# One score matmul for two chunks in recurrence levels 1 to 16, with half of each half's tokens in turned order

## The chip, the cores and the metric

The kernel runs on one core of one Trainium2 chip. The metric is the device time of one execution in microseconds (us); the time of a kernel is the median of its runs. The engines are PE (matrix multiply, with PEld for the loading of its weights), DVE (vector), ACT (scalar), POOL (general) and SP (which issues most DMAs). Each engine works off its own list of instructions in order and waits on semaphores for the others.

## The reference

A decoder layer for 2048 tokens of width 1024: two groups of heads in parallel on the normed input, an output projection, and a gated MLP with a causal convolution. What matters here is the recurrence of the first group, four heads with keys and values of width 128, in chunks:

```python
def step(state, inp):
    qi, ki, vi, gi = inp
    b = jnp.cumsum(gi, axis=2)
    rel = b[:, :, :, None, :] - b[:, :, None, :, :]
    decay = jnp.exp(jnp.where(causal, rel, -jnp.inf))
    scores = jnp.einsum('bhtk,bhsk,bhtsk->bhts', qi, ki, decay)
    intra = jnp.einsum('bhts,bhsv->bhtv', scores, vi)
    inter = jnp.einsum('bhtk,bhkv->bhtv', qi * jnp.exp(b), state)
    ...
    return new_state, intra + inter
```

A score of query t and key s is a sum over 128 channels, each weighted with the decay of that channel between s and t. The second group is attention of eight heads with a window of 128 tokens.

## The kernel before, in words

Activations stand transposed, channels on the 128 partitions and tokens along the free axis. The kernel goes through the 2048 tokens in two halves of 1024 (`hf`). In each half a mixing stage comes first: for each head `h` of 0 to 3, `hgrn` computes the recurrence and `attend` two heads of attention, both written as generators whose pieces the main loop calls in turn. After it come the output projection (`out_proj`, tile `pop`), the MLP (`gate_up`, `down`). Projections go through `unit` (L195): weights and activations are split into a high and a low part, and three matmuls of 128x512 stand for each pair of tiles. `project_v` (tile `pvv`, matmuls of 256 columns) makes the values for two heads at a time, beside heads 0 and 2.

In `hgrn` the scores of a chunk of 128 tokens are built by levels m = 1, 2, 4, ... 64. At level m the tokens are cut into pairs of blocks of m: queries of the later block meet keys of the earlier one. For that the kernel keeps Q and K with the decay inside the block already multiplied in, and F with the decay of whole blocks. Per level (L445 to L475):

- for m < 32, PE multiplies, for each of the 8 chunks, all 128 keys of the chunk as weights (`K`, float32) with the 64 queries of the later blocks (L454). The result `plev` is 128x64 a chunk, one PSUM bank for the 8; only the places where key block and query block belong together are wanted;
- DVE multiplies the later blocks of Q (L462) and the earlier blocks of K (L463) by F, which prepares the next level, and forms the next F (L465);
- DVE copies the wanted places, given by the mask `lmask`, from `plev` into the scores `ST` (L470, a predicated copy);
- levels 32 and 64 have blocks of their own (L460) and are copied by ACT (L474).

The diagonal (`pdiag`, L428) comes before, the transposes of K (`pkn`), the state products (`pu`, L491) and the output (`po`) after.

The matmuls of a level read Q and K before DVE overwrites them, and those of the next level read what DVE wrote. `plev` comes from a pool of two PSUM banks. The order on each engine isn't that of the code: the framework's scheduler sets it when the kernel is built, and puts projection or attention work between the levels. In head 3 of each half little is left for that: the first output projections (`pop`), the attention scores (`psc`), and their transposes (`ppt`, `poT`).

Of the kernel before, what the change touches and what calls it, by code (L numbers as in the profile page):

```python
# [45 lines left out]
def hymba_layer(ctx: ExitStack, tc: tile.TileContext, a: dict, out: bass.AP):  # L46
# [49 lines left out]
    def constants():  # L96
# [10 lines left out]
        for m in LEVELS[:5]:  # L107
            t = cp.tile([P, 64], F32, name=f"lmask{m}")
# [4 lines left out]
            nc.gpsimd.affine_select(out=t, in_=t, compare_op=ALU.is_ge, fill=0.0, base=m - 1,  # L113
                                    pattern=[[2 * m, nb], [0, m]], channel_multiplier=-1)
            C.lmask[m] = t
# [146 lines left out]
    def load(hf, X, stage, W=None):  # L262

        st = Stats(inv_tile())
        for kt in range(KT):
            first = W is not None and kt == 0
            if W is not None and kt < 2:
                W.append(prep(a["w_att"][ATT_J + kt], parts=(slice(0, P), slice(P, D)) if first else (slice(0, D),)))
            x = stage()
            X.append(new_x())  # L270
            for c in [bs for _, bs in halves()] if first else [slice(0, HALF)]:
                nc.sync.dma_start(x[:, c], a["xT"][kt, :, hf * HALF + c.start:hf * HALF + c.stop])
                split(x[:, c], nmw[:, kt:kt + 1], dst=[t[:, c] for t in X[kt]])
            st.add(x)
            yield st

    def first_unit(X, W, i, then={}):
        return unit(W[i] if W else a["w_att"][ATT_J + i], X, "kv", then=then)

    def rows(kv):  # L280
        return slice(kv * HD, (kv + 1) * HD)

    def att_keys(hf, kv, invb, p):
# [10 lines left out]
        for jj, dst in ((ATT_J, kT), (ATT_J + 1, vT)):  # L294
            o = kv[jj - ATT_J]
            for b, bs in halves():
                nc.vector.tensor_tensor(dst[:, bs], o[b], invb[:, bs], op=ALU.mult)
                nc.scalar.activation(dst[:, bs], dst[:, bs], AF.Identity, bias=C.battn[:, jj:jj + 1])
# [15 lines left out]
    def attend(hf, j, X, invb, KS, V, mix, p):  # L314
# [3 lines left out]
        for b, bs in halves():  # L318
            nc.vector.scalar_tensor_tensor(qT[:, bs], o[b], 0.125, invb[:, bs], op0=ALU.mult, op1=ALU.mult)
            nc.scalar.activation(qT[:, bs], qT[:, bs], AF.Identity, bias=C.bq[:, j:j + 1])  # L320
# [83 lines left out]
    def hgrn(hf, h, X, invb, vs, WG, mix, p, fu=None):  # L404
# [28 lines left out]
        def gate():  # L433
            gu = unit(WG.get(h, a["w_g"][h]), X, "g")
            s = p.tile([P, HALF], F32, tag="f", name="sg", bufs=2)
            for b, bs in halves():
                nc.vector.tensor_tensor(q[:, bs], gu[b], invb[:, bs], op=ALU.mult)
                nc.scalar.activation(s[:, bs], q[:, bs], AF.Sigmoid)
                nc.vector.tensor_tensor(q[:, bs], q[:, bs], s[:, bs], op=ALU.mult)
# [5 lines left out]
        for m in LEVELS:  # L445
            nb = HALF // (2 * m)
            nbc = 64 // m
            Qv = Q.rearrange("p (b w m) -> p b w m", w=2, m=m)
            Kv = K.rearrange("p (b w m) -> p b w m", w=2, m=m)
            Fv = F.rearrange("p (b w) -> p b w", w=2)  # L450
            pl = ps("hg", "plev")
            if m < 32:
                for c in range(TT):
                    mm = nc.tensor.matmul(pl[:, c * 64:(c + 1) * 64], K[:, c * P:(c + 1) * P],  # L454
                                          Qv[:, c * nbc:(c + 1) * nbc, 1], start=True, stop=True)
# [6 lines left out]
            nc.vector.tensor_tensor(Qv[:, :, 1], Qv[:, :, 1], Fv[:, :, 0:1].to_broadcast([P, nb, m]), op=ALU.mult)  # L462
            nc.vector.tensor_tensor(Kv[:, :, 0], Kv[:, :, 0], Fv[:, :, 1:2].to_broadcast([P, nb, m]), op=ALU.mult)  # L463
            Fn = p.tile([P, nb], F32, tag=f"F{m}", name=f"F{m}", bufs=1)
            nc.vector.tensor_tensor(Fn, Fv[:, :, 0], Fv[:, :, 1], op=ALU.mult)  # L465
            F = Fn
            if m < 32:
                dst = ST.rearrange("p c (b w m) -> p c b w m", w=2, m=m)[:, :, :, 1]
                mk = C.lmask[m].bitcast(U32).rearrange("p (b m) -> p b m", m=m)
                nc.vector.copy_predicated(dst, mk.unsqueeze(1).to_broadcast([P, TT, nbc, m]),  # L470
                                          pl.rearrange("p (c b m) -> p c b m", c=TT, m=m))
                continue
# [529 lines left out]
def _layout(i):  # L1002
# [3 lines left out]
    def cols(w, idx):  # L1006
# [54 lines left out]
```

## Time and profile before

| | us |
|---|---|
| runs of the kernel, three | 2253.62, 2253.84, 2255.33 |
| median | 2253.84 |
| the profiled execution: span from first to last instruction (it has no other time of its own) | 2251.9 |
| PE idle in the span (span less busy time) | 38.0 |
| level matmuls L454, busy (640 records) | 83.5 |
| Q and K products L462 and L463 of all levels, busy | 76.9 |
| predicated copies L470, busy (40) | 38.0 |

A profile comes from one execution, recorded by the hardware. Busy time of matmuls overlaps, since they are pipelined: how long a group holds PE is read from the start of its first matmul to the start of the next work. A float32 matmul leaves two records, each with a weight load. "Granted clock" is the share of its full clock that PE was given.

### The profile page before, as it was taken

To read this page: it belongs to the slowest core of one execution; us is meant where nothing else is said; L and a number is where in the kernel's file an instruction comes from. 1 tells how busy PE (TensorE), PEld (TensorE's weight loads), DVE (VectorE), ACT (ScalarE), POOL (GpSimd) and SP (SyncE) were. 2 spreads that over 40 slices of the span, in tenths; PEclk is the share of its full clock that TensorE was granted. 3 is DMA by queue.
4 is the path that set the end of the run, shared out by engine and by line. 5 is a ranking of instruction groups with operands and counts; after the bars stand their busy time and mean duration, and the time that the engine had idled before them with its cause. 6 is when DMAs were issued, how large, how long until landed. Compare 5 with 4: busy or idle time off the path is not lost.

```text
span 2251.9 us, 29785 instructions
## 1 busy us (share of the span) xinstructions
PE 2213.9 (98%) x11622; PEld 1862.1 (83%) x11622; DVE 1639.2 (73%) x2458; ACT 1024.6 (45%) x1781; POOL 7.2 (0%) x27
## 2 busy tenths in 40 slices
PE   8999999999999999999999999999999999999997
PEld 6988987778888888888889889887788888888887
DVE  6567467688888887885855665676888878887766
ACT  5345344454444444435724344435544444443353
POOL 1000000000000000000000000000000000000000
PEclk9999998999999999999999999989999999999999
DMA  4101002222323234974630101113232322359643
GB/s 151 38 29 38 29 29 75 94 85 84 118 88 122 89 122 134 360 254 148 207 122 29 38 29 29 53 51 121 67 114 97 115 92 98 107 179 390 225 136 127
DMA packets 89997, 254.19 MB, mean 113 GB/s; under 512 B 11008, under 2 KB 13184, under 8 KB 89856
## 3 DMA queue, kind: packets, MB, share of 16 engines
q1 hardware_dynamic: 87552, 251.17, 32.6%
q8 instruction: 91, 1.49, 0.3%
q10 hardware_dynamic: 2304, 1.12, 0.2%
q14 instruction: 50, 0.41, 0.1%
HBM read 195.10 MB, written 57.15 MB: 112 GB/s over the span
## 4 chain that ended last, share of the span: by engine, by line
PE 92%; DVE 4%; ACT 2%; DMA 2%; issue 1%; SPq 0%; DVEq 0%; ACTq 0%
PE X L674 7%; PE X L675 7%; PE X L676 7%; PE pop L195 6%; PE hq L195 4%; PE q L195 4%; PE f L195 4%; PE g L195 4%; PE Y L674 3%; PE Y L675 3%; PE Y L676 3%; PE pdx L856 3%; PE pdx L858 3%; PE pdx L857 3%; PE plev L454 3%; PE pdy L857 3%
## 5 line engine op out<-in xcount | busy, mean ns | idle before, releaser
L551 ACT CAST whi<-raw 128x1024 fp32r<-128x1024 f32 x88 | 92.6, 1053 | 118.6 <-PE X L675 72.8
L675 PE MATMUL X<-T,whi 128*128 128x512 f32 x352 | 137.8, 391 | 0.0
L674 PE MATMUL X<-T,whi 128*128 128x512 f32 x352 | 137.2, 390 | 0.0
L676 PE MATMUL X<-T,wlo 128*128 128x512 f32 x352 | 137.0, 389 | 0.0
L740 DVE SCALAR_TENSOR_TENSOR y<-ga,cw,y 128x1024 f32<-128x1024 f32 x88 | 112.6, 1280 | 25.4 <-ACT y L738 25.3
L176 ACT CAST whi<-raw 128x1024 fp32r<-128x1024 f32 (+2 forms) x61 | 63.0, 1036 | 123.8 <-PE q L195 59.1
L552 DVE TENSOR_TENSOR wlo<-raw,whi 128x1024 fp32r<-128x1024 f32 x88 | 107.3, 1219 | 0.0
L680 ACT COPY u<-X 128x512 f32<-128x512 f32 x88 | 51.6, 586 | 113.0 <-PE X L676 112.8
L552 DVE TENSOR_TENSOR xld<-raw,xhd 128x1024 fp32r<-128x1024 f32 x72 | 80.9, 1132 | 22.4 <-ACT xhd L551 22.0
L454 PEld LDWEIGHTS plev<-Q,K 128*128 128x128 f32 x640 | 82.8, 206 | 9.3 <-DVE K L463 4.5
L551 ACT CAST xhd<-raw 128x1024 fp32r<-128x1024 f32 x72 | 69.6, 978 | 45.9 <-DMA raw<-act0T 17.6
L454 PE MATMUL plev<-Q,K 128*128 128x64 f32 x640 | 83.5, 287 | 6.1 <-DVE K L463 6.1
L195 PE MATMUL pop<-XL,whi 128*128 128x512 f32 x256 | 84.5, 395 | 0.7 <-DVE XL L207 0.7
L195 PE MATMUL pop<-XH,wlo 128*128 128x512 f32 x256 | 84.4, 394 | 0.8 <-DVE wlo L177 0.8
L195 PE MATMUL pop<-XH,whi 128*128 128x512 f32 x256 | 84.3, 400 | 0.2
L462 DVE TENSOR_TENSOR Q<-Q,F 128x512 f32<-128x512 f32 x48 | 33.1, 690 | 67.9 <-PE plev L454 39.1
L177 DVE TENSOR_TENSOR wlo<-raw,whi 128x1024 fp32r<-128x1024 f32 (+2 forms) x61 | 73.0, 1202 | 9.3 <-ACT whi L176 9.2
L674 PEld LDWEIGHTS X<-T,whi 128*128 128x128 f32 x352 | 66.1, 188 | 14.2 <-ACT u L680 0.6
L676 PEld LDWEIGHTS X<-T,wlo 128*128 128x128 f32 x352 | 66.1, 188 | 14.2 <-issue 0.5
L675 PEld LDWEIGHTS X<-T,whi 128*128 128x128 f32 x352 | 66.1, 188 | 14.0 <-issue 0.5
L856 PE MATMUL pdx<-xhd,hid 128*128 128x512 f32 x192 | 74.5, 391 | 1.9 <-ACT hid L551 1.0
L674 PE MATMUL X<-T,Sh 128*128 128x512 f32 x176 | 70.1, 398 | 5.2 <-ACT s L680 5.2
(356 smaller groups left out, 6603.0 us busy)
## 6 DMA issues: line engine op xcount, KB each, us to landing
wr<-in_w_down SPq DMA_DIRECT2D x90, 512.0 KB, 5.5
raw<-in_w_gate SPq DMA_DIRECT2D x44, 512.0 KB, 3.6
raw<-in_w_up SPq DMA_DIRECT2D x44, 512.0 KB, 3.6
raw<-act0T SPq DMA_DIRECT2D x20, 512.0 KB, 6.5
raw<-act1T SPq DMA_DIRECT2D x20, 512.0 KB, 5.0
act0B<-y SPq DMA_DIRECT2D x33, 256.0 KB, 2.4
act1B<-y SPq DMA_DIRECT2D x33, 256.0 KB, 2.4
raw<-in_w_out SPq DMA_DIRECT2D x16, 512.0 KB, 4.0
```

Of the source, the lines that this page charges most:

```text
L177: nc.vector.tensor_tensor(lo[:, c], raw[:, c], hi[:, c].bitcast(F32), op=ALU.subtract)
L195: nc.tensor.matmul(o[b], w, x[:, bs], start=f, stop=l)
L454: mm = nc.tensor.matmul(pl[:, c * 64:(c + 1) * 64], K[:, c * P:(c + 1) * P], Qv[:, c * nbc:(c + 1) * nbc, 1], start=True, stop=True)
L551: nc.scalar.copy(h, src)
L552: (eng or nc.vector).tensor_tensor(l, src, h.bitcast(F32), op=ALU.subtract)
L674: nc.tensor.matmul(o, wh[:, ws], xh, start=i == 0 and not more, stop=False, skip_group_check=more)
L675: nc.tensor.matmul(o, wh[:, ws], xl, start=False, stop=False, skip_group_check=more)
L676: nc.tensor.matmul(o, wl[:, ws], xh, start=False, stop=i == 3, skip_group_check=more)
L740: nc.vector.scalar_tensor_tensor(y, g[:, w:w + HALF], C.cw[:, ft, w:w + 1], y, op0=ALU.mult, op1=ALU.add)
L856: nc.tensor.matmul(o, wh[:, i, c], ah[:, i, cols], start=f, stop=False, skip_group_check=more)
L857: nc.tensor.matmul(o, wh[:, i, c], al[:, i, cols], start=False, stop=False, skip_group_check=more)
L858: nc.tensor.matmul(o, wl[:, i, c], ah[:, i, cols], start=False, stop=l, skip_group_check=more)
```

## The change

It has four parts.

1. The input of each half is permuted on the host (`xP`): of its second 512 tokens each block of 32 is turned, so that token r stands at place 31 - r. The order of the blocks stays. What leaves the recurrence or feeds attention (keys, values, queries, gates, and the output `pot`) is turned back while DVE evacuates it from PSUM, by a view with a negative step (`blocks`). Levels 32 and 64 see whole blocks and stay as they were.
2. In a turned block the earlier keys of a pair stand in the second place and the later queries in the first. So in chunk u of the first 512 tokens and chunk u + 4 of the second the wanted keys lie in opposite blocks. ACT gathers them into one tile `G` (128 keys, 64 of each chunk, for each of 4 pairs of chunks), and one matmul takes these as weights and the 64 queries of both chunks as 128 columns: 4 matmuls a level in place of 8. `G` has two buffers.
3. The masks get a second side, the products of Q and K take the blocks of both kinds in one instruction each, K now before Q.
4. The scratch area of dynamic DMA is set to 2048.

```diff
+            t = cp.tile([P, 2, 64], F32, name=f"lmask{m}")
...
-            nc.gpsimd.affine_select(out=t, in_=t, compare_op=ALU.is_ge, fill=0.0, base=0,
-                                    pattern=[[-2 * m, nb], [0, m]], channel_multiplier=1)
-            nc.gpsimd.affine_select(out=t, in_=t, compare_op=ALU.is_ge, fill=0.0, base=m - 1,
-                                    pattern=[[2 * m, nb], [0, m]], channel_multiplier=-1)
+            for side in range(2):
+                ts = t[:, side]
+                nc.gpsimd.affine_select(out=ts, in_=ts, compare_op=ALU.is_ge, fill=0.0, base=-side * m,
+                                        pattern=[[-2 * m, nb], [0, m]], channel_multiplier=1)
+                nc.gpsimd.affine_select(out=ts, in_=ts, compare_op=ALU.is_ge, fill=0.0, base=m - 1 + side * m,
+                                        pattern=[[2 * m, nb], [0, m]], channel_multiplier=-1)
...
-                nc.sync.dma_start(x[:, c], a["xT"][kt, :, hf * HALF + c.start:hf * HALF + c.stop])
+                nc.sync.dma_start(x[:, c], a["xP"][kt, :, hf * HALF + c.start:hf * HALF + c.stop])
...
+    def blocks(t, turn=False):
+        v = t.rearrange("p (g r) -> p g r", r=32)
+        return v[:, :, ::-1] if turn else v
+
+    def across(t, base, dims):
+        v = t[:, :]
+        return bass.AP(v.tensor, v.offset + base, [list(v.ap[0])] + dims)
...
-                nc.vector.tensor_tensor(q[:, bs], gu[b], invb[:, bs], op=ALU.mult)
+                nc.vector.tensor_tensor(blocks(q[:, bs], b), blocks(gu[b]), blocks(invb[:, bs]), op=ALU.mult)
...
             if m < 32:
-                for c in range(TT):
-                    mm = nc.tensor.matmul(pl[:, c * 64:(c + 1) * 64], K[:, c * P:(c + 1) * P],
-                                          Qv[:, c * nbc:(c + 1) * nbc, 1], start=True, stop=True)
-                marks[m] = mm
+                n, nu = 64 // m, TT // 2
+                far, near = [[512 - m, 2], [P, nu], [2 * m, n], [1, m]], [[512 + m, 2], [P, nu], [2 * m, n], [1, m]]
+                G = p.tile([P, 512], F32, tag="G", name="G", bufs=2)
+                nc.scalar.copy(across(G, 0, [[m, 2], [P, nu], [2 * m, n], [1, m]]), across(K, 0, near))
+                for u in range(nu):
+                    marks[m] = nc.tensor.matmul(across(pl, u * 64, [[256, 2], [1, 64]]), G[:, u * P:(u + 1) * P],
+                                                across(Q, u * P + m, [far[0]] + far[2:]), start=True, stop=True)
+                nf = P // m
+                Kv, Qv = across(K, 0, near), across(Q, m, far)
+                Fk = across(F, 1, [[4 * nf - 1, 2], [nf, nu], [2, n], [0, m]])
+                Fq = across(F, 0, [[4 * nf + 1, 2], [nf, nu], [2, n], [0, m]])
+                nc.vector.tensor_tensor(Kv, Kv, Fk, op=ALU.mult)
+                nc.vector.tensor_tensor(Qv, Qv, Fq, op=ALU.mult)
...
-                dst = ST.rearrange("p c (b w m) -> p c b w m", w=2, m=m)[:, :, :, 1]
-                mk = C.lmask[m].bitcast(U32).rearrange("p (b m) -> p b m", m=m)
-                nc.vector.copy_predicated(dst, mk.unsqueeze(1).to_broadcast([P, TT, nbc, m]),
-                                          pl.rearrange("p (c b m) -> p c b m", c=TT, m=m))
+                mk = C.lmask[m].bitcast(U32).rearrange("p s t -> p (s t)")
+                nc.vector.copy_predicated(across(ST.rearrange("p c t -> p (c t)"), m, far),
+                                          across(mk, 0, [[64, 2], [0, nu], [m, n], [1, m]]),
+                                          pl.rearrange("p (s u b m) -> p s u b m", s=2, u=nu, m=m))
...
-            nc.vector.scalar_tensor_tensor(g[:, bs], pt, C.hgw, g[:, bs], op0=ALU.mult, op1=ALU.mult)
+            nc.vector.scalar_tensor_tensor(blocks(g[:, bs]), blocks(pt, b), C.hgw, blocks(g[:, bs]),
+                                           op0=ALU.mult, op1=ALU.mult)
...
+        "xP": x[np.where(ar(S) // 512 % 2, ar(S) ^ 31, ar(S))].T.reshape(KT, P, S),
...
-    nc = bacc.Bacc("TRN2", target_bir_lowering=False, num_devices=1)
+    nc = bacc.Bacc("TRN2", target_bir_lowering=False, num_devices=1, dynamic_dma_scratch_size=2048)
```

Keys, values and queries of attention are evacuated through `blocks` in the same way as the gate above.

What the scheduler made of it is shown at two places. The first is head 0 of the first half, from the diagonal on. DVE before the change (each row: line, operation, written tile, read tiles, size; `hg` and `f` tiles are the head's, `att` and `ql` the attention's, `wlo` a weight split):

```order
L429 TENSOR_TENSOR ST<-pdiag,ident 128x512 x2
L462 TENSOR_TENSOR Q<-Q,f 128x512
L463 TENSOR_TENSOR K<-K,f 128x512
L470 COPY_PREDICATED ST<-lmask_287,plev 128x512
L319 SCALAR_TENSOR_TENSOR att_700<-q_650,invb 128x512
L319 SCALAR_TENSOR_TENSOR att_700<-q_651,invb 128x512
L177 TENSOR_TENSOR wlo<-raw,whi 128x1024
L332 TENSOR_TENSOR ql<-att_700,qh 64x512
L462 TENSOR_TENSOR Q<-Q,F_548 128x256x2
L463 TENSOR_TENSOR K<-K,F_548 128x256x2
```

DVE there with the change:

```order
L442 TENSOR_TENSOR ST<-pdiag,ident 128x512 x2
L473 TENSOR_TENSOR K<-K,f 128x2x256
L473 TENSOR_TENSOR K<-K,F_556 128x2x128x2
L474 TENSOR_TENSOR Q<-Q,f 128x2x256
L491 COPY_PREDICATED ST<-lmask_287,plev 128x2x256
L473 TENSOR_TENSOR K<-K,F_568 128x2x64x4
L331 SCALAR_TENSOR_TENSOR att_700<-q_650,invb 128x512
L331 SCALAR_TENSOR_TENSOR att_700<-q_651,invb 128x16x32
L179 TENSOR_TENSOR wlo<-raw,whi 128x1024
L474 TENSOR_TENSOR Q<-Q,F_556 128x2x128x2
L491 COPY_PREDICATED ST<-lmask_293,plev 128x2x128x2
```

The K products have moved one level or two ahead of the Q products, and the second evacuation of a query tile is in blocks of 32. ACT at the same place with the change (the copies `G<-K` are new, the rest stood there in nearly the same order):

```order
L320 COPY V<-pv 128x512
L178 CAST whi<-raw 128x1024
L465 COPY G<-K 128x2x128x2
L465 COPY G<-K 128x2x64x4
L178 CAST whi<-raw 128x1024
L333 ACTIVATE att_700<-att_700,bq 128x512 x2
L343 CAST qh<-att_700 64x512
L344 CAST qh<-att_700 64x512
L465 COPY G<-K 128x2x32x8
L343 CAST qh<-att_700 64x512
L344 CAST qh<-att_700 64x512
```

The copies for m = 2 and 4 stand together, ahead of the level that uses them. On PE this head had 32 `pvv` matmuls between two level groups; it has 27 now.

The second place is head 3 of the first half, from the Q product of the second level on. DVE before the change (`sc`, `m`, `es` and `den` belong to the softmax of attention):

```order
L462 TENSOR_TENSOR Q<-Q,F_3112 128x256x2
L463 TENSOR_TENSOR K<-K,F_3112 128x256x2
L470 COPY_PREDICATED ST<-lmask_291,plev 128x256x2
L358 TENSOR_TENSOR m<-m,sinkb 128x8
L360 TENSOR_TENSOR es<-sinkb,m 128x8
L368 TENSOR_TENSOR den<-den,es 128x8
L361 TENSOR_SCALAR m<-m 128x8
L369 RECIPROCAL den<-den 128x8
L370 TENSOR_TENSOR sc<-sc,den 128x1024
L462 TENSOR_TENSOR Q<-Q,F_3126 128x128x4
```

DVE there with the change, from the first Q product on:

```order
L474 TENSOR_TENSOR Q<-Q,f 128x2x256
L209 TENSOR_TENSOR XL<-att_2214,XH 128x1024
L491 COPY_PREDICATED ST<-lmask_287,plev 128x2x256
L365 COPY_PREDICATED sc<-own,psc 128x256
L452 TENSOR_TENSOR hg_2912<-hg_2912,sg 128x512
L365 COPY_PREDICATED sc<-own,psc 128x256
L452 TENSOR_TENSOR hg_2912<-hg_2912,sg 128x512
L473 TENSOR_TENSOR K<-K,F_3090 128x2x128x2
L371 TENSOR_TENSOR m<-m,sinkb 128x8
L474 TENSOR_TENSOR Q<-Q,F_3090 128x2x128x2
L491 COPY_PREDICATED ST<-lmask_293,plev 128x2x128x2
L365 COPY_PREDICATED sc<-own,psc 128x256 x2
```

Behind these stand the softmax's `es`, and then the K product, the Q product and the predicated copy of the third level. The normalisation of `sc`, which stood between the second and the third Q product, has moved behind the levels of m = 4 and 8.

More of the change, by code (lines that the diff above doesn't have):

```diff
@@ L296, in att_keys @@
             for b, bs in halves():
-                nc.vector.tensor_tensor(dst[:, bs], o[b], invb[:, bs], op=ALU.mult)
+                nc.vector.tensor_tensor(blocks(dst[:, bs], b), blocks(o[b]), blocks(invb[:, bs]), op=ALU.mult)
                 nc.scalar.activation(dst[:, bs], dst[:, bs], AF.Identity, bias=C.battn[:, jj:jj + 1])
@@ L318, in attend @@
         for b, bs in halves():
-            nc.vector.scalar_tensor_tensor(qT[:, bs], o[b], 0.125, invb[:, bs], op0=ALU.mult, op1=ALU.mult)
+            nc.vector.scalar_tensor_tensor(blocks(qT[:, bs], b), blocks(o[b]), 0.125, blocks(invb[:, bs]),
+                                           op0=ALU.mult, op1=ALU.mult)
             nc.scalar.activation(qT[:, bs], qT[:, bs], AF.Identity, bias=C.bq[:, j:j + 1])
@@ L461, in hgrn @@
                                          Q[:, c * P + s0 + m:c * P + s0 + 2 * m], start=True, stop=True)
-            nc.vector.tensor_tensor(Qv[:, :, 1], Qv[:, :, 1], Fv[:, :, 0:1].to_broadcast([P, nb, m]), op=ALU.mult)
-            nc.vector.tensor_tensor(Kv[:, :, 0], Kv[:, :, 0], Fv[:, :, 1:2].to_broadcast([P, nb, m]), op=ALU.mult)
+                Fv = F.rearrange("p (b w) -> p b w", w=2)
+                nc.vector.tensor_tensor(Qv[:, :, 1], Qv[:, :, 1], Fv[:, :, 0:1].to_broadcast([P, nb, m]), op=ALU.mult)
+                nc.vector.tensor_tensor(Kv[:, :, 0], Kv[:, :, 0], Fv[:, :, 1:2].to_broadcast([P, nb, m]), op=ALU.mult)
+            Fv = F.rearrange("p (b w) -> p b w", w=2)
             Fn = p.tile([P, nb], F32, tag=f"F{m}", name=f"F{m}", bufs=1)
@@ L523, in hgrn @@
                 nc.tensor.transpose(pt[:, i * P:(i + 1) * P], on[:, 4 * b + i], ident)
-            nc.vector.scalar_tensor_tensor(g[:, bs], pt, C.hgw, g[:, bs], op0=ALU.mult, op1=ALU.mult)
+            nc.vector.scalar_tensor_tensor(blocks(g[:, bs]), blocks(pt, b), C.hgw, blocks(g[:, bs]),
+                                           op0=ALU.mult, op1=ALU.mult)
             if h == HG - 1:
```

7 lines of the change are left out of this document (2 added, 5 removed).

## The prediction

> **What bounds the kernel now.** I read the page's busy table first, then the busy time by stage, then who waited for whom.
>
> ```profile
> span 2251.9 us, 29785 instructions
> PE 2213.9 (98%) x11622; PEld 1862.1 (83%) x11622; DVE 1639.2 (73%) x2458; ACT 1024.6 (45%) x1781; POOL 7.2 (0%) x27
> ```
> ```profile
> 56.00:120.00 64.00, 64.00 (x488) 59.58 (x487) 34.47 (x61) 23.73 (x50) 0.00 (x0) 1.00 0.11 34
> 360.00:420.00 60.00, 54.76 (x371) 46.55 (x370) 37.01 (x78) 16.33 (x63) 0.00 (x0) 0.89 0.06 18
> 1480.00:1540.00 60.00, 58.13 (x373) 48.12 (x372) 36.80 (x78) 18.38 (x65) 0.00 (x0) 0.89 0.07 20
> ```
> ```profile
> PE plev L454 <- DVE K L463: 6.1, 5, 2.7
> ```
>
> PE is busy for 98% of the span. The second fence is the busy time of PE, weight loads, DVE, ACT and POOL by stretch, then the granted clock and the DMA share. In 56 to 120 us, where head 0 runs its levels, PE never stops and DVE is busy for 34.47 of 64 us. So there a microsecond taken from PE is a microsecond of span. In the stretches of head 3 of each half (360 to 420 and 1480 to 1540), which I call the tails, PE has gaps and its mean clock is 0.89. The third fence says that the level matmuls waited for DVE's K product only 6.1 us in all. Hence two sums: 30 level groups of heads 0 to 2 in both halves on a saturated PE, and 10 in the two tails.
>
> **What the change takes from PE.** The next rows are PE and weight loads in order of time: start, length, kind, count. Each float32 matmul leaves two records.
>
> ```profile
> 63.66 1.95 PE L428 MATMUL pdiag<-hg,K 128*128 128x128 f32 x16
> 65.36 0.71 PE L195 MATMUL q<-XH,wlo 128*128 128x512 f32 x2
> ...
> 69.77 1.89 PE L454 MATMUL plev<-Q,K 128*128 128x64 f32 x16
> 71.47 0.48 PE L195 MATMUL q<-XH,wlo 128*128 128x512 f32 x1
> ```
> ```profile
> 401.20 1.09 PE L491 MATMUL pu<-v,Kn 128*128 128x128 f32 x8
> 402.05 0.47 PE L195 MATMUL pop<-XL,whi 128*128 128x512 f32 x1
> ```
>
> A level's group of 8 matmuls (16 records, 64 columns each) holds PE from 69.77 to 71.47, 1.70 us. The `pdiag` group, 16 records with the same weights and twice the columns, holds it from 63.66 to 65.36: 1.70 us too. So a group's length goes with the number of weight loads, not with its columns up to 128. The new group is 4 matmuls, 8 records, of 128 columns; `pu` of that shape took 401.20 to 402.05, 0.85 us. Saved: 1.70 - 0.85 = 0.85 us a group. There are 2 halves x 4 heads x 5 levels = 40 groups: **34.0 us** of PE, 25.5 in heads 0 to 2 and 8.5 in the tails.
>
> One thing the rows don't show: 128 columns read with gaps (every second block of m words) and written in two runs of 64. The old 64-column reads had the same gaps and could have hidden a rate up to half of the dense one under the weight load. So the new group lies between 0.85 (dense, as `pu`) and 1.70 us (half rate), which saves 34.0 or nothing. I take 0.85, since at m = 4 to 16 the runs are long and the instruction is otherwise `pu`'s.
>
> [...]
>
> **What it adds.** The rows are DVE's in the first tail, in order of time, then its predicated copies of m = 2 and m = 4 in head 0.
>
> ```profile
> 362.48 1.22 DVE L207 TENSOR_TENSOR XL<-att,XH 128x1024 fp32r<-128x1024 f32 x1
> 363.61 0.45 DVE L352 COPY_PREDICATED sc<-own,psc 128x256 f32<-128x256 uint32 x1
> 363.94 0.69 DVE L439 TENSOR_TENSOR hg<-hg,sg 128x512 f32<-128x512 f32 x1
> 364.55 0.16 DVE L358 TENSOR_TENSOR m<-m,sinkb 128x8 f32<-128x8 f32 x1
> 364.62 0.45 DVE L352 COPY_PREDICATED sc<-own,psc 128x256 f32<-128x256 uint32 x1
> 364.96 0.69 DVE L462 TENSOR_TENSOR Q<-Q,f 128x512 f32<-128x512 f32 x1
> 365.56 0.69 DVE L463 TENSOR_TENSOR K<-K,f 128x512 f32<-128x512 f32 x1
> 366.16 1.30 DVE L470 COPY_PREDICATED ST<-lmask,plev 128x512 f32<-128x512 uint32 x1
> 367.24 0.73 DVE L439 TENSOR_TENSOR hg<-hg,sg 128x512 f32<-128x512 f32 x1
> ```
> ```profile
> 78.48 1.31 DVE L470 COPY_PREDICATED ST<-lmask,plev 128x512 f32<-128x512 uint32 x1
> ...
> 84.08 0.71 DVE L470 COPY_PREDICATED ST<-lmask,plev 128x512 f32<-128x512 uint32 x1
> ```
> ```profile
> L680 ACT COPY u<-X 128x512 f32<-128x512 f32 x88 | 51.6, 586 | 113.0 <-PE X L676 112.8
> L437 DVE TENSOR_TENSOR hg<-g,invb 128x512 f32<-128x512 f32 x16 | 10.6, 678 | 0.2 <-PE g L195 0.2
> 4.70 3.15 POOL L113 TENSOR_SCALAR_AFFINE_SELECT lmask<-lmask 128x64 f32<-128x64 f32 x5
> ```
>
> - *The copy G on ACT.* 40 copies of 128x512 at 586 ns (L680) are 23.4 us, 2.9 a head. No row has a two-word stride on ACT; the nearest with broken runs is L470, 1.30 us at m = 1, so 23 to 52 us. I take 0.6 each. ACT has 23.73 of 64 us in the first stretch and takes them beside PE.
> - *New waits.* K's product must wait for the copy that reads old K, and the next matmul for that copy. Behind a waiting K product on DVE stand the Q product, the predicated copy and weight splits that PE needs. In head 0 the order leaves 27 `pvv` matmuls between groups, where it left 32. These start 0.12 us apart, so a group comes every 27 x 0.12 + 0.85 = 4.1 us instead of 5.5. DVE's own share of a level is Q 0.60, K 0.60 and the predicated copy 1.1 to 1.2 (about 0.6 for m of 4 and more): 2.4 us at most. K runs a level ahead of Q in the new order, so copy and K product (1.2 us) lie beside the previous group. I charge nothing; were this cover gone, each level would lose what its chain exceeds 4.1 by.
> ```profile
> 73.17 0.28 PE L543 MATMUL pvv<-whi,XH 128*128 128x256 f32 x1
> 73.29 0.27 PE L544 MATMUL pvv<-whi,XL 128*128 128x256 f32 x1
> ```
> - *Turned blocks.* 28 evacuations (two of keys and values, four of queries, four of gates, four of `pot` in each half) read or write backwards in blocks of 32. Forwards they cost 0.68 (L437). Backwards may cost nothing more, or, as the two forms of L470 differ, 0.6 each: 17 us of DVE. DVE's idle time in the heads hides it; in a tail two stand on its path, 0 to 1.2 us. I take 0.
> - *K and Q products, F products, masks.* As many elements, runs as long: no price. POOL gets 10 more selects; its last five took 3.15 us to 7.85, so it ends near 13 us, and no mask is wanted before the first level group, at 69.77. The inputs read `xP` instead of `xT`, equal in size, on the same queue. The smaller DMA scratch area answers to no row; DMA is busy for 11% or less of the three stretches above, and I price it at nothing.
>
> **The tails.** PE's rows of the first, then its stretches of 5 us.
>
> ```profile
> 365.14 0.28 PE L343 MATMUL psc<-KS,ql 128*128 128x256 f32 x1
> 366.30 2.00 PE L454 MATMUL plev<-Q,K 128*128 128x64 f32 x16 [0.89 <-DVE K L463]
> 371.00 3.65 PE L454 MATMUL plev<-Q,K 128*128 128x64 f32 x16 [2.70 <-DVE K L463]
> 374.44 1.91 PE L379 MATMUL ppt<-ident,sc 128*128 128x128 f32 x8
> 376.14 3.63 PE L454 MATMUL plev<-Q,K 128*128 128x64 f32 x16
> 379.53 1.20 PE L195 MATMUL pop<-XH,whi 128*128 128x512 f32 x2
> ```
> ```profile
> 365.00:370.00 5.00, 2.41 (x20) 2.07 (x18) 5.00 (x10) 3.37 (x11) 0.00 (x0) 0.83 0.28 94
> 370.00:375.00 5.00, 4.00 (x19) 4.04 (x20) 4.08 (x10) 4.37 (x24) 0.00 (x0) 0.50 0.00 0
> 375.00:380.00 5.00, 5.00 (x24) 4.86 (x23) 4.97 (x10) 0.71 (x4) 0.00 (x0) 0.50 0.02 3
> 380.00:385.00 5.00, 5.00 (x28) 3.43 (x27) 2.24 (x4) 0.00 (x0) 0.00 (x0) 0.80 0.00 0
> ```
>
> DVE is full from 365 to 370, PE waits 0.89 and 2.70 us for K, and the clock falls to 0.50 until 382: two level groups take twice their 1.7 us. From the end of Q's first product (365.56) to the fourth group (376.14) are 10.6 us. In the new order DVE has between the end of that product and that of the third Q product: XL 1.13, predicated 1.1, two sc 0.68, two gate 1.2, K and Q of m = 2 1.2, predicated 1.1, two sc 0.68, K and Q of m = 4 1.2, small ones 0.15: 8.4 us. So the fourth group starts 2.1 us sooner. PE has the second and third group, four `pop` and eight `psc` in these 8.4 us, under 4 us of work, so it still idles near 5, and I let the clock fall again. To the end of the fourth group it was 379.53 - 365.56 = 14.0 us; it becomes 8.5 and a group at half clock, 1.7: 10.2, 3.8 sooner. Three groups of 0.85 of that stand in the sum already, so 1.2 lies beyond it; the waits of transposes and `poT` for DVE behind it, which no row prices, may take some back: I take **+1 a tail**. The ends: the clock stays up, then the fourth group takes 0.85 and the first `pop` (1.20 us a pair at 379.53, against 0.71 at 65.36) lose nothing, 2 more, +3; or idling as long again as 0.89 + 2.70 us comes behind, with a little of it at half clock, -4.
>
> [...]
>
> **The sum.** 25.5 + 8.5 + 2 = 36 us off a span of 2251.9: 2215.9. The profiled execution gives only its span; the median of the runs, 2253.84, lies 1.9 above it. So 2253.84 - 36 = **2217.8 us**.
>
> **The rivals.**
> - *A, slower:* the levels outside the tails begin to wait. For: K product and copy now hand over between DVE and ACT, each in order. Against: the 4.1 us against 2.4 above. One spell as in the tail costs 0.89 + 2.70 idle and about 5 at half clock (two groups and `ppt`), 8.6 us; 36 / 8.6 makes 4.2 spells the point where it decides. One in each of the six heads: 6 x 8.6 - 36 = 15.6 slower, 2269. Chance 0.05.
> - *B, no gain:* reads with gaps or two-run writes go at half rate; the group stays 1.70, tails and waits as now: 2252. Nothing in the rows excludes it. Chance 0.05. Only m = 1 and 2 slow: 16 x 0.85 = 13.6 is lost, 2231. Chance 0.05.
> - *C, worse tails:* -4 instead of +1 each, for DVE is as full as before and only its order is new: 2253.84 - 34 + 8 = 2228. Chance 0.06.
> - *D, better tails:* the clock stays up, +3 each: 2253.84 - 34 - 6 = 2214. For it: the new groups keep PE's columns twice as dense. Chance 0.08.
> - *That it doesn't do what it says* is out: the order shows 4 matmuls in place of 8.
>
> **The numbers.** The forecast, 2217.8 within 6, has 0.71. The range leaves out A and B (0.10) and ends beyond C, D and the partial B, which, with 0.2 us a group more or less (8 us over 40), reach 2206 and 2236. A run of this kernel can be told from no change at about 0.2%, 4.5 us. Faster by that: all but A and B, 0.90; same 0.05; slower 0.05.
>
> **What would show it.** 320 records of the level matmuls where there were 640, groups of 8 in 0.85 us; no wait on the copy in 56 to 120 us; the fourth group of each tail some 2 us sooner after Q's first product; PE's busy time down by some 34. A group of 1.2 us or more, half clock outside the tails, or ACT's copies named by PE's waits would make it wrong.

## The result, and the profile after

| | median | runs | |
|---|---|---|---|
| before, on the same chip | 2253.95 us | 2253.62 to 2255.33 | |
| with the change | 2216.91 us | 2216.09 to 2224.03 | ratio 0.9844, 95% interval 0.983 to 0.9857 |

The ratios here and below are estimated with their intervals and differ a little from the quotients of the medians. The forecast was 2217.8. The profiled execution took 2216.09 us, its span is the first line of the page, its busy table the second:

```profile
span 2214.4 us, 29214 instructions
PE 2173.3 (98%) x11302; PEld 1818.8 (82%) x11302; DVE 1637.8 (74%) x2458; ACT 1047.8 (47%) x1821; POOL 13.0 (1%) x37
```

The page's groups: line, engine, operation, count, then total busy time and mean, then idle time before them and what ended it. Behind them the whole-span table of who waited for whom (total, times, longest):

```profile
L467 PE MATMUL plev<-Q,G 128*128 128x128 f32 x320 | 44.0, 280 | 6.6 <-DVE Q L474 4.5 <-ACT G L465 1.9
L465 ACT COPY G<-K 128x512 f32<-128x512 f32 x40 | 25.5, 639 | 69.5 <-DVE K L473 32.0 <-PE plev L467 28.1 <-DVE K L431 9.1
```
```profile
PE plev L467 <- DVE Q L474: 4.5, 4, 2.0
PE plev L467 <- ACT G L465: 1.9, 1, 1.9
```

PE lost 40.6 us of busy time (2213.9 to 2173.3; 34 was forecast, and the tails' time at half clock counts as busy too), the level records went from 640 to 320, and ACT got its 40 copies. PE's rows in order of time show a new group in head 0, from its start to that of the next matmul:

```profile
69.15 1.07 PE L467 MATMUL plev<-Q,G 128*128 128x128 f32 x8
69.97 0.48 PE L197 MATMUL q<-XH,wlo 128*128 128x512 f32 x1
```

That is 0.82 us. The forecast was 0.85, and all 30 groups of the heads, m = 1 and 2 among them, hold PE for 0.81 to 0.86.

To see where the time went I cut both profiles at the same instructions: heads 0 to 2 (first `pdiag` of a half to the third head's `pot`), the tail (to the last `po`), and the rest of the half. These are the stretches' lengths and busy times, engines as in the prediction. Before:

```profile
63.70:354.40 290.70, 290.70 (x2016) 257.22 (x2015) 176.75 (x338) 131.97 (x328) 0.00 (x0) 1.00 0.13 40
354.40:409.50 55.10, 49.51 (x360) 42.59 (x359) 37.86 (x69) 20.69 (x68) 0.00 (x0) 0.88 0.10 30
409.50:1176.80 767.30, 763.23 (x3366) 626.67 (x3366) 601.44 (x804) 357.07 (x490) 0.00 (x0) 1.00 0.43 149
1176.80:1466.10 289.30, 289.30 (x2011) 255.30 (x2010) 175.18 (x330) 132.14 (x326) 0.00 (x0) 1.00 0.12 38
1466.10:1522.60 56.50, 52.99 (x380) 45.84 (x379) 38.71 (x70) 21.86 (x70) 0.00 (x0) 0.88 0.11 37
1522.60:2242.50 719.90, 711.47 (x3257) 589.85 (x3255) 561.58 (x762) 325.59 (x458) 0.00 (x0) 1.00 0.42 143
```

With the change:

```profile
63.00:342.50 279.50, 279.50 (x1887) 243.43 (x1887) 175.32 (x336) 139.93 (x342) 0.00 (x0) 1.00 0.14 41
342.50:392.30 49.80, 43.19 (x327) 36.53 (x326) 38.38 (x70) 23.72 (x74) 0.00 (x0) 0.93 0.11 34
392.30:1157.80 765.50, 761.66 (x3366) 625.62 (x3365) 601.48 (x804) 358.21 (x491) 0.00 (x0) 1.00 0.44 149
1157.80:1438.60 280.80, 280.80 (x1900) 244.63 (x1899) 174.73 (x331) 140.69 (x342) 0.00 (x0) 1.00 0.13 40
1438.60:1487.70 49.10, 41.57 (x331) 34.67 (x330) 37.72 (x70) 23.84 (x74) 0.00 (x0) 1.00 0.12 34
1487.70:2204.80 717.10, 709.61 (x3257) 588.95 (x3256) 562.11 (x762) 325.74 (x458) 0.00 (x0) 1.00 0.42 144
```

| stage | saved | forecast |
|---|---|---|
| heads 0 to 2, both halves | 11.2 + 8.6 = 19.8 (20.8) | 25.5 |
| tails | 5.4 + 7.3 = 12.6 (11.7) | 8.5 + 2 |
| rest of the halves | 1.8 + 2.9 = 4.7 | 0 |
| up to the first `pdiag` | 0.6 | 0 |

The numbers are of unrounded starts. In brackets they are corrected for work that crossed the border of a stage: some 0.84 us of `psc` (8 records) went from the heads of the first half into its tail, 1.81 us of `pop` from the second tail into its heads. So the total is as forecast, but its parts are not: the heads gave 5 us too little, the rest about 5 that nobody had asked for. The experiments look for both.

### The profile page after: what moved, and what is told of

Read it like the earlier page. It is cut to its first block, busy times and chain, and to the rows that moved or that the text cites. A ratio compares the mean times of both kernels' runs of the same rounds, so it can differ in the third digit from the quotient of the medians.

```text
span 2214.4 us, 29214 instructions
## 1 busy us (share of the span) xinstructions
PE 2173.3 (98%) x11302; PEld 1818.8 (82%) x11302; DVE 1637.8 (74%) x2458; ACT 1047.8 (47%) x1821; POOL 13.0 (1%) x37
## 4 chain that ended last, share of the span: by engine, by line
PE 94%; DVE 3%; ACT 1%; DMA 1%; issue 0%; SPq 0%; DVEq 0%; ACTq 0%
PE X L697 7%; PE X L698 7%; PE X L699 7%; PE pop L197 6%; PE hq L197 4%; PE f L197 4%; PE q L197 4%; PE g L197 4%; PE pdx L879 4%; PE pdx L880 4%; PE pdx L881 4%; PE Y L697 4%; PE Y L699 4%; PE Y L698 4%; PE pdy L880 3%; PE pdy L879 3%
## 5 line engine op out<-in xcount | busy, mean ns | idle before, releaser
L179 DVE TENSOR_TENSOR wlo<-raw,whi 128x1024 fp32r<-128x1024 f32 (+2 forms) x61 | 73.2, 1204 | 13.2 <-ACT whi L178 13.2
L880 PE MATMUL pdx<-xld,hid 128*128 128x512 f32 x192 | 74.8, 390 | 0.0
L881 PE MATMUL pdx<-xhd,lod 128*128 128x512 f32 x192 | 73.7, 389 | 0.0
L567 PE MATMUL pvv<-whi,XL 128*128 128x256 f32 x256 | 73.1, 287 | 0.0
```

What stands on the lines that cost most here:

```text
L179: nc.vector.tensor_tensor(lo[:, c], raw[:, c], hi[:, c].bitcast(F32), op=ALU.subtract)
L567: nc.tensor.matmul(o[:, 0:256], xl[:, t], hi[:, c], start=False, stop=False)
L880: nc.tensor.matmul(o, wh[:, i, c], al[:, i, cols], start=False, stop=False, skip_group_check=more)
L881: nc.tensor.matmul(o, wl[:, i, c], ah[:, i, cols], start=False, stop=l, skip_group_check=more)
```

## The experiments

"Held" below is a sum over PE's rows in order of time: from the start of a kind of matmul to the start of the next row, so that it holds the idle time and the switch behind it too.

**The weight loads.** Layout, copies and turned blocks stay, and each matmul is split in two again.

```diff
                 for u in range(nu):
-                    marks[m] = nc.tensor.matmul(across(pl, u * 64, [[256, 2], [1, 64]]), G[:, u * P:(u + 1) * P],
-                                                across(Q, u * P + m, [far[0]] + far[2:]), start=True, stop=True)
+                    for s in range(2):
+                        marks[m] = nc.tensor.matmul(across(pl, u * 64 + s * 256, [[1, 64]]), G[:, u * P:(u + 1) * P],
+                                                    across(Q, u * P + m + s * (512 - m), far[2:]), start=True, stop=True)
```

> Each merged matmul of 128 columns is made two of 64 columns with the same weights; layout, gathered buffer and order of Q and K stay. Theory (a level group costs its count of weight loads and records, not its columns): 16 records take 1.70 us again in place of 0.83, 40 groups x 0.87 = 34.8 us, the total comes to 2245 to 2254 us, about that of the kernel before. Rival 1 (the columns or the layout made the gain): the group stays near 0.85 us and the total at 2217. Rival 2 (layout, gathered copies and turned views have a price that the merging pays for): the group returns to 1.70 but the total exceeds the kernel before by over 3 us, 2257 or more.

Median 2245.31 us, ratio to before 0.9972 (0.9955 to 0.999). Its group in head 0 is back at 1.70 us (69.58 to 71.28):

```profile
69.58 1.89 PE L468 MATMUL plev<-Q,G 128*128 128x64 f32 x16
71.28 0.48 PE L197 MATMUL q<-XH,wlo 128*128 128x512 f32 x1
```

So the gain hangs on the count of matmuls, not on columns or layout. (Each brings two records and two weight loads; no run here tells a price of the record from one of the load.) Rival 2 falls: with the old count the layout is not dearer than the kernel before but 8 us cheaper by the medians. Most of that, some 7 us when corrected for work that crossed the border, lies in the second tail, where its profile shows no fall of the clock and that of the kernel before one of 13.65 us. Against the changed kernel `plev` is held 13.1 and 13.2 us longer in heads 0 to 2 of the two halves, yet `poT` and `po` 1.4 and 1.9 us shorter. So `poT` and `po`, which nobody edited, were dearer when the level groups were short.

**The attention's groups in pieces.** In heads 0 to 2 the new order issues `poT` in 16 and 18 pieces where the old had 13 and 14; held went from 12.29 to 13.47 us and from 13.10 to 14.44, though its work is the same. `po`, `pu` and `pkn` together were held 1.2 and 2.4 us longer. PE's rows with the change show such a piece alone, between `q` and `pkn`:

```profile
209.29 0.43 PE L403 MATMUL poT<-po,V 128*64 128x128 f32 x2
209.65 0.66 PE L506 MATMUL pkn<-ident,K 128*128 128x128 f32 x4
```

It holds PE for 0.36 us; two records of an unbroken group take 0.12 (32 are held 1.90 us). The next experiment makes `poT` begin with the product that DVE finishes last, so that the scheduler has the whole group ready at once.

```diff
-                for prev in range(1 if noprev else 2):
-                    for kv in range(2):
+                for prev in (0,) if noprev else (1, 0):
+                    for kv in (1, 0):
                         r = rows(kv)
                         nc.tensor.matmul(oT[r, i * P:(i + 1) * P], V[:, n + 1 - prev, r], pm[kv][prev][:, i],
-                                         start=prev == 0, stop=noprev or prev == 1)
+                                         start=noprev or prev == 1, stop=prev == 0)
```

> The attention's output matmuls poT begin with the product that DVE makes last (previous chunk, second key head), so that a group of 32 records is ready as a whole and is not issued in pieces; no instruction is added. Theory (in the heads the new order cuts poT, po and pu into more pieces and each piece costs 0.1 to 0.2 us more, which is what is missing of the 12.75 us of each half): poT of heads 0 to 2 takes 12 us or less in place of 13.5 and 14.4, and the total falls by 1 to 4 us, to 2213 to 2216. Rival (the records cost what they cost, pieces or not, and what is missing was lost elsewhere): total 2216 to 2218, within 0.5 us of the changed kernel. A second rival (groups start later, and PE or DVE waits for them): 2218 or more.

PE's rows of the same place now show 22 of the group's 28 records in one stretch, four of them in 0.22 us (the other six still follow in two pieces):

```profile
209.40 0.39 PE L403 MATMUL poT<-pp,V 128*64 128x128 f32 x4
209.62 0.39 PE L403 MATMUL poT<-po,V 128*64 128x128 f32 x4
209.84 0.39 PE L403 MATMUL poT<-pp,V 128*64 128x128 f32 x4
```

And its heads, against 279.50 and 280.80:

```profile
63.00:338.60 275.60, 275.60 (x1887) 242.98 (x1886) 175.93 (x337) 140.34 (x342) 0.00 (x0) 1.00 0.14 42
1155.10:1432.60 277.50, 277.50 (x1907) 244.59 (x1906) 174.18 (x331) 141.40 (x343) 0.00 (x0) 1.00 0.13 41
```

`poT` is held 11.23 and 12.05 us in 8 and 9 pieces, 2.2 and 2.4 less; the heads are 3.8 and 3.2 us shorter with no instruction added or taken away, and PE waits in neither kernel. The rest of that gain stands at `po` and at projections (`q`, `hq`, `f`), which the edit does not name. The total is 2214.99 us, ratio 0.9831 (0.9816 to 0.9846): its interval overlaps that of the change, since the second tail became 2.8 us longer, in an execution with a mean granted clock of 0.993 where that of the change had 0.996. So the heads show that pieces cost time; the total alone does not show it.

The same edit in the kernel before tells whether the missing 5 us are these pieces or belong to the levels:

> The kernel before with whole poT groups. Theory (pieces of poT cost the same in either kernel; the changed kernel had more of them): poT of heads 0 to 2 falls from 12.29 and 13.10 us to about 11.2 and 12.1 as with the change, heads 0 to 2 by 1 to 2 us in each half, and the difference of the two kernels with whole groups, heads 0 to 2 of both halves, comes to 25.5 us, as forecast, give or take 1.5. Rival (the missing 5 us belong to the new form of the levels itself): this kernel gains as much as the changed one, 3.2 to 3.8 us in each half, and the difference stays at 20 to 21.

Median 2246.53 us, ratio 0.9967 (0.9957 to 0.9978). `poT` is held 10.74 and 11.40 us in 10 pieces each, somewhat less than expected. Its heads are 3.7 and 0.4 us shorter (corrected for `psc` and `pop` that crossed their border, 2.1 and 3.3):

```profile
63.90:350.90 287.00, 287.00 (x2005) 255.28 (x2004) 176.09 (x337) 131.64 (x327) 0.00 (x0) 1.00 0.12 40
1173.40:1462.30 288.90, 288.90 (x2027) 257.53 (x2027) 176.00 (x331) 132.87 (x328) 0.00 (x0) 1.00 0.12 39
```

With the edit in both kernels, the change saves 11.4 + 11.4 = 22.8 us in the heads, and 23.2 when corrected, as above, for 0.46 us of `pop` that `b_whole` leaves to its first tail. That is neither expectation: it lies between the theory's 24 to 27 and the rival's 20 to 21. Pieces of `poT` explain some 2.4 of the missing 4.7 us. What is left shows as `pu` (1.1 us), `poT` (1.1) and `pkn` (0.4), held longer still; these are float32 groups that now stand next to each other. PE's rows show that the neighbours make the price. The same 8 records of `pu` stand between projections in the kernel before with the edit, and between pieces of `poT` in the changed kernel with it:

```profile
310.64 1.05 PE L491 MATMUL pu<-v,Kn 128*128 128x128 f32 x8
311.45 0.47 PE L195 MATMUL hq<-XL,whi 128*128 128x512 f32 x1
```
```profile
210.58 1.16 PE L513 MATMUL pu<-v,Kn 128*128 128x128 f32 x8
211.67 0.32 PE L403 MATMUL poT<-pp,V 128*64 128x128 f32 x1
```

They are held 0.81 and 1.09 us. Wherever such places occur in the heads of the 13 profiles, the prices repeat to 0.01 us, whatever the kernel: 8 records of `pu` cost 0.81 between projections and 1.09 between pieces of `poT`, 16 of them 1.70 and 1.98, 4 of `pkn` 0.35 and 0.58. Why PE takes longer at such a border is not shown.

**The copies.** ACT writes each G twice.

```diff
                 nc.scalar.copy(across(G, 0, [[m, 2], [P, nu], [2 * m, n], [1, m]]), across(K, 0, near))
+                nc.scalar.copy(across(G, 0, [[m, 2], [P, nu], [2 * m, n], [1, m]]), across(K, 0, near))
```

> The gathered copy is written twice by ACT, 40 more copies of 0.62 us, 24.8 us of ACT work. Theory (a copy has cover beside PE in the heads; only in the two tails the 3rd and 4th group of each wait for it): 0 to 2.5 us more, 2217 to 2219.5. Rival (ACT delivers just in time, the copies stand on the way to the matmuls everywhere): up to 24.8 us more, 2230 to 2242.

Median 2224.11 us, ratio 0.987 (0.9852 to 0.9889), more than the theory's 2219.5 and below the rival's range; the changed kernel itself took 2222.26 us in its one run beside it. The heads are 278.57 and 279.16 us, no longer than with one copy; the first tail is 0.9 us longer, the second 5.3:

```profile
1438.30:1492.80 54.50, 46.83 (x337) 39.48 (x336) 38.07 (x70) 25.89 (x78) 0.00 (x0) 0.87 0.11 37
```

1.1 us of that is `pop` from the heads. The mean clock of this tail is 0.87 where it was 1.00; in the first tail it is 0.93 with one copy and with two. A copy is hidden in the heads, as forecast. Both expectations left out the clock, which in this tail differs between two executions of the changed kernel as well (1.00 and 0.97, below); that the second copy made it fall is not shown.

**The tails.** The second unit of the output projection may be issued only behind the level group of m = 8. PE's rows of the two tails with the change, third group, fourth group and what follows:

```profile
357.61 1.13 PE L467 MATMUL plev<-Q,G 128*128 128x128 f32 x8 [1.22 <-DVE Q L474]
360.68 2.04 PE L467 MATMUL plev<-Q,G 128*128 128x128 f32 x8 [1.95 <-ACT G L465]
362.38 1.20 PE L197 MATMUL pop<-XH,whi 128*128 128x512 f32 x2
...
1453.73 1.13 PE L467 MATMUL plev<-Q,G 128*128 128x128 f32 x8 [1.21 <-DVE Q L474]
1456.82 1.13 PE L467 MATMUL plev<-Q,G 128*128 128x128 f32 x8 [1.96 <-DVE Q L474]
1457.71 0.71 PE L197 MATMUL pop<-XH,whi 128*128 128x512 f32 x2
```

The 5 us around the start of the fourth group have a granted clock (the last number but two) of 0.50 in the first tail and 1.00 in the second:

```profile
360.00:365.00 5.00, 4.32 (x14) 3.85 (x15) 4.46 (x10) 3.21 (x14) 0.00 (x0) 0.50 0.00 0
1455.00:1460.00 5.00, 3.18 (x18) 2.83 (x19) 5.00 (x10) 4.56 (x20) 0.00 (x0) 1.00 0.00 0
```

The same waits, 1.2 and 1.95 us, cost the clock in one tail and not in the other. The edit lets `pop` start one group sooner:

```diff
-AFTER = {1: 8, 2: "po"}
+AFTER = {1: 4, 2: "po"}
```

> The changed kernel with the second unit of the output projection allowed after the level group of m = 4, not m = 8, so that its matmuls can stand between the third and the fourth group of a tail. Theory (in the tails PE is idle for DVE's products at the third and fourth group, 3 us in each tail, and the idle spell lets the clock fall): the wait at the fourth group goes, the clock stays above 0.9, and the total falls by 2 to 6 us, to 2211 to 2215. Rival (the tail is as long as DVE's chain of levels: what PE does earlier it waits for later): within 1 us of the changed kernel, 2216 to 2218, with the idle time showing at a later level or at po.

Median 2213.03 us, ratio 0.9814 (0.98 to 0.9829). The tails, in place of 49.80 and 49.10 us:

```profile
344.70:390.50 45.80, 41.01 (x328) 34.62 (x327) 37.83 (x70) 23.69 (x74) 0.00 (x0) 1.00 0.11 36
1436.40:1483.30 46.90, 41.39 (x331) 34.53 (x330) 38.36 (x70) 23.64 (x74) 0.00 (x0) 1.00 0.11 35
```

The wait at the fourth group is gone and both tails are shorter, so the rival (DVE's chain sets the tail's length) falls. The heads repeat at 279.46 and 280.77 us.

**Two more profiles, and the scratch area.**

> The changed kernel once more, for a second profile. If the stages are what the program makes them: the two mixing stages, their heads and the MLP stages repeat to within 0.5 us each, the first unit's X products outside the mixing stage take as long as before, and the total is 2216 to 2218 us. Rival: the 4.5 us that the MLP stages were shorter than in the profile of the kernel before are a variation from run to run; then these stages come out 1 us or more longer this time. For the clock: if its fall in the tail of the first half (4th level group 2.04 us) and its staying up in the tail of the second (1.13 us) are chance, one of them changes.

> The kernel before once more, for a second profile. If the MLP stages are shorter with the change for a reason in the program, they take 767 us (after the first half) and 720 us (after the second) again. Rival (a variation from run to run, as between the two profiles of the changed kernel, where they differed by 0.7 and 1.0 us): one of them comes out 1 us or more shorter. Heads 0 to 2 should repeat at 290.7 and 289.3 us whichever holds, since PE never waits there.

> The kernel before with the scratch area of dynamic DMA set to 2048, nothing else. Theory (the kernel's transfers do not use it): the same program and the same time as before, within 0.2%. Rival (it changes the transfers or where tiles lie, and with them the MLP stages): 2 us or more shorter, outside the mixing stages.

The changed kernel again: 2222.26 us, heads 279.46 and 280.76 (as in the first profile), rest of the halves 766.20 and 718.05 (0.7 and 1.0 longer), the second tail 1.6 longer, its clock 0.97 where it was 1.00, and 3.7 us more up to the first `pdiag`: PE waited 1.8 us longer for the first inputs, and its first matmuls of 512 columns, which start 0.43 us apart where later ones start 0.23 apart, went on until 17.6 us in place of 11.2. The kernel before again: 2253.54 us, heads 290.70 and 289.30, rest 766.97 and 719.83. With the small scratch area: 2252.88 us, ratio 0.9994 (0.9985 to 1.0003), so that part of the change is worth nothing that can be seen.

The rest of a half has the same instructions in all these kernels, and its length still differs. Much of the difference stands behind one wait. PE's row of it and the stretches around it, before:

```profile
487.56 0.63 PE L674 MATMUL X<-T,Sh 128*128 128x512 f32 x1 [2.62 <-ACT s L680]
```
```profile
480.00:490.00 10.00, 7.38 (x28) 5.73 (x27) 10.00 (x16) 7.70 (x13) 0.00 (x0) 0.89 0.44 153
490.00:500.00 10.00, 9.79 (x48) 7.75 (x48) 7.95 (x19) 4.18 (x9) 0.00 (x0) 0.94 0.01 4
```

With the change:

```profile
470.38 0.50 PE L697 MATMUL X<-T,Sh 128*128 128x512 f32 x1 [2.64 <-ACT s L703]
```
```profile
462.00:472.00 10.00, 7.36 (x33) 5.80 (x32) 10.00 (x16) 8.51 (x15) 0.00 (x0) 1.00 0.42 132
472.00:482.00 10.00, 9.79 (x51) 7.84 (x50) 9.45 (x24) 4.69 (x9) 0.00 (x0) 1.00 0.07 27
```

The wait is as long, but in the kernel before the clock fell with it, for 3.41 us (the two stretches lose 0.11 and 0.06 of 10 us at half clock), and with the change it did not. Each half has this wait once, so the 13 profiles hold 26 of them. In 17 the clock fell: these stages took 766.3 to 767.7 us in the first half and 718.05 to 720.14 in the second. In 9 it stayed up: 765.2 to 766.2 and 717.0 to 717.7. The groups do not overlap, and their means lie 1.5 and 1.8 us apart; half of 3.41 is 1.7. The first profile of before has the fall in both halves, that of the change in neither.

What decides it can be read from the granted clock in narrow stretches. In each of the 13 executions every change of the clock, down to its last fall, comes a whole multiple of 3.41 us after the first rise (that is where the first matmuls pass from 0.43 to 0.23 us, at 10 to 18 us). So in these executions the clock changed on a grid of 3.41 us only, and the grid lay elsewhere in each. In the 17 cases with a fall a point of this grid lies near the end of the wait, between 0.56 us before it and 1.11 behind; in the 9 others the nearest lies at least 0.70 before it or 1.58 behind. So in these 26 cases the same wait cost the clock or did not by where it met the grid.

**Both edits together.**

> Both edits: whole poT groups, and the projection's second unit after m = 4. Theory (they act at different places, heads and tails): their gains add, 7 us from the heads as the profile with whole groups shows, 2 to 6 from the tails, 2205 to 2211 us. Rival (the order of the tail changes with either, and a gain in the heads is given back there, as in the second tail with whole groups, 2.8 us longer): 2212 to 2216.

> The changed kernel with whole groups and the projection's second unit after m = 2. Theory (the tail's idle time before the third group goes as well, 1.2 us in each tail, with it the spell that lets the clock fall): 2206 to 2210 us. Rival (the levels are DVE's chain, and PE only moves its idle time to the transposes and poT behind, as it did in the second tail with both edits): 2209 to 2214.

> The kernel before with both edits, whole poT groups and the projection's second unit after m = 4. Theory (the edits help it less: it has fewer pieces to join, and its tails have less room): 2246 to 2251 us, so that the change is worth 37 to 41 us between kernels with both edits. Rival (they help it as much, 6 to 7 us): 2247 or less and a change worth no more than 37.

| both edits | median | ratio to before |
|---|---|---|
| on the change, `pop` after m = 4 | 2210.27 us | 0.9803 (0.9789 to 0.9816) |
| on the change, `pop` after m = 2 | 2208.46 us | 0.98 (0.9787 to 0.9814) |
| on the kernel before, after m = 4 | 2242.52 us | 0.9955 (0.9942 to 0.9969) |

On the change the gains add, and 2208.46 us is the shortest median here; whether m = 2 beats m = 4 is inside the intervals. In the profile of m = 2 the tails are 47.6 and 47.4 us. The median lies in the theory's range, but the largest share of PE's idle time there (2.9 of 7.0 and 3.2 of 7.9 us) now stands before `ppt` and `poT`, as the rival said. The kernel before gains as much from the edits (0.0045 of 2253, 10 us) as the changed one (0.0041, 9 us), so its theory falls; its rival, which expected 6 to 7, put it too low. Between kernels with both, the change is worth 0.9955 - 0.9803 of 2253, about 34 us, give or take some 4 by the intervals.

## Why the forecast was right, step by step

- *PE saturated in heads 0 to 2, so a microsecond of PE is one of span.* Right: PE is busy for all of both stretches in every one of these profiles.
- *A group costs its weight loads, 0.85 us, 40 times.* Right in the price, 0.81 to 0.86 in the heads; that it is the load and not the record that costs was not told apart. `plev` is held 13.0 us less in each half's heads, forecast 12.75. Splitting the matmuls alone brings 1.70 back. Rival B, whole or for m = 1 and 2, is out. Reading with gaps and writing two runs of 64 words had no price that shows: 0.82 us, against 0.85 for `pu`, which writes one run.
- *Heads 25.5 us.* Too large by 5. The step that failed is an unspoken one: that all other matmuls keep their price. The level groups themselves gave 26.0, half a microsecond more than forecast. The order changed around them, and float32 groups that were issued whole came in pieces and beside others. Joining the pieces of `poT` in both kernels brings the change to 23.2. What separates that from 26.0 is the price of the neighbours, 2.7 us at `pu`, `poT` and `pkn`: 8 records of `pu` cost 1.09 us between pieces of `poT` and 0.81 between projections.
- *G copies, new waits, turned blocks nothing.* Right in the heads: even two copies each make them no longer. The copies took 0.64 us on the mean. One of the prediction's signs against itself did show: PE's waits name ACT's copy, once, for 1.9 us, at the fourth group of the first tail, where the sum had let PE idle. In the heads PE never waits. Turned blocks cost nothing on DVE: of the 16 evacuations of each kind half are turned, and their least, median and greatest times (ns) lie close together.

```profile
L331 DVE SCALAR_TENSOR_TENSOR att<-q,invb x16: 667/684/692, 72.6 to 1422.6; 128x512 f32<-128x512 f32 x16
L546 DVE SCALAR_TENSOR_TENSOR hg<-pot,hgw,hg x16: 742/747/753, 149.0 to 1497.7; 128x512 f32<-128x512 f32 x16
```

- *Tails 4.25 + 1 each.* 11.7 us corrected in place of 10.5: 6.2 in the first, 5.5 in the second. In the first it went as worked out: the fourth group came 8.6 us behind the end of Q's first product (8.5 worked out, 10.5 before), at half clock, 1.70 us from start to start. In the second the clock stayed up, which is rival D; it was given 0.08 as if it held for both tails or neither, but each falls by itself, and the repeated profile had a fall of 3.41 us in both. That denser columns keep the clock up, D's argument, is shown by no run: the first tail has the same groups, and its clock fell to 0.50. Nor did D's price of 3 us show: the second tail gave no more than the first, and PE idled 7.4 us in it where it had idled 3.5.
- *Elsewhere nothing.* The program does nothing there, right; the two profiles differ by 4.7 us all the same, and falls of the clock that one had and the other had not account for some 3.3 (1.5 + 1.8); the rest is not explained. Those falls are luck as far as the 26 waits show, since each went by where the grid lay. The kernel before had the fall in 6 of 6 such waits over its three profiles (one with the small scratch area); all the others in 11 of 20. But its two waits lie 326.1 steps of 3.41 us apart, so both meet the grid at nearly the same place, and the six are no more than three draws. That the program makes the fall likelier is not shown.
- *The sum.* 36 was forecast and 37.5 is the difference of the spans: 5 too much in the heads, 1 too little in the tails, 5 too little elsewhere and at the start. The forecast was good to 0.9 us; its terms were good to 5, and that they made up for each other is luck.

## What to carry to other kernels

Here a float32 matmul of 64 columns held PE as long as one of 128, 0.21 us for its two records, so two that read half of their weights in vain could become one, since a cheap layout brought the wanted halves together. Where PE is saturated, count what a shorter group does to the order of the others as well: pieces and neighbours of float32 groups had a price here (0.36 us for two records of `poT` in place of 0.12, 1.09 for eight of `pu` in place of 0.81). A group that waits for two producers should begin with the one that comes last, or the scheduler may deal it out in pieces. And before a stage that the edit does not touch is credited or blamed for a few microseconds, look at the granted clock behind each idle spell of PE: here it fell at 17 of 26 spells of about 2.62 us, for 3.41 us in 16 of them, and at 9 it did not.

## What the runs showed of the hardware

The clock fell, for 3.41 us and once for 6.83, at a single idle spell of about 2.62 us (2.62 and 2.64 in the rows above) in 17 of 26 cases and did not in 9, in the same instructions. In the changed kernel's first profile the two tails have idle spells of 1.2 and 1.95 us at the same level groups; the clock fell for 6.83 us in one tail and not at all in the other. In its second profile it fell for 3.41 us in each. In each of the 13 profiled executions it changed only at whole multiples of 3.41 us after its first rise. That rise came at another time in each, 9.9 us into the span in the first profile of before and 11.2 in that of the change.

Two records of a float32 group whose weights have 64 columns (`poT`) held PE for 0.36 us alone and for 0.12 within an unbroken group of 32, with no idle time shown in either. Eight records of `pu` (128 columns) held it for 0.81 us between projections and for 1.09 between such pieces.
